# Layer 0's dense work in three passes, with unsplit weights, in place of two

## The chip, the cores and the metric

One core of one Trainium2 chip runs the whole program. The metric is the device time of one execution in microseconds (us). The kernel before took 3567.16 us (median of three runs, 3563.05 to 3572.27).

## The reference, cut to what matters

A decoder trunk of two layers over 512 tokens of 1024 features, in float32. Each layer has a token mixer and then a product-key retrieval of single experts:

```python
m  = x @ w_in                      # q, k, v | RG-LRU branch, its gate | 2 merge gates
ya = diff_attention(q, k, v, ...)  # 8 heads, two causal softmax maps each
yr = rg_lru(conv4(xr)) * gelu(gr)  # a recurrence along the tokens
y  = sigmoid(ga) * (ya @ w_br_attn) + sigmoid(gr) * (yr @ w_br_lru)
x  = layer_norm(alpha * x + y @ w_out)
# PEER: 8 heads x 16 of 16384 experts for each token
s1, i1 = top_k(q1 . keys1, 16); s2, i2 = top_k(q2 . keys2, 16)
e, g   = top 16 of the 256 sums s1 + s2, softmax over them
x  = layer_norm(alpha * x + sum_j g_j * gelu(x . u[e_j]) * v[e_j])
```

Every token needs 128 rows of `u` and of `v`, each of 1024 floats, in each layer. The tokens are causal: attention and the recurrence of a block of 128 tokens need the blocks before it, not those behind it. An expert phase needs only its own block's tokens and their choice.

## The kernel before, in words

The 512 tokens are four blocks of 128. Two streams of work are issued into one program (`run`, L752): `gathers()` and `dense()`.

**Gathers.** For each layer and block, `experts` (L682) issues 128 gathers (L730): one gather fetches, for each of 128 tokens, one row of `uv` (8 KB, `u` and `v` side by side), 1 MB in all, into one of 8 buffers (`self.gp`). There are 2 x 4 x 128 = 1024 gathers, numbered here from 0; gather 128 is the first of block 1. VectorE takes the dot product of the `u` half (L733), small operations on VectorE and ScalarE make a weight `w`, and the `v` half times `w` is added either by VectorE (`acc`, L703) or by TensorE (a diagonal of `w` on ScalarE at L707, then the product `pv` at L709). `self.share` sets which: a share of 0.7 means that seven of ten value rows go to VectorE.

**Dense work.** A pass over some blocks is `mixer` (L529 on: transposes, `attention` and `lru` woven together, two `merge`s, the output projection, a layer norm), then `route` (the scores and the choice of experts of the pass's first block), then `route_late` (the choice for its other blocks). A pass loads the layer's whole weights anew, chunk by chunk of 512 KB (`weight`, L195), whatever the number of its blocks: 80 chunks in the mixer (8 each for q, k, v, xr, gr, two gates, two branches, the output) and 16 in `route`. A chunk is 8 matmuls against activations of as many columns as the pass has tokens (`proj_T`, L220) or 8 for each block (`proj_N`, L242). Weights pass through 5 buffers.

**The first pass** (blocks 0 and 1 of layer 0) is special. Nothing can be gathered before its first experts are chosen. It is made with split operands: each weight chunk becomes two float32r parts (`split_weight`, L200: a copy on ScalarE, L204, a subtraction on VectorE, L205), activations likewise (`keep`), and a product is three passes of float32r matmuls, 24 to a chunk in place of 8.

**What sets the order.** `PLAN` (L53) gives for each pass the span of gathers over which it is spread: the gather at which the mixer starts, by which it ends and the scores begin, by which the first block's choice ends, by which the others' does. `run` steps whichever stream is behind. The framework then orders each engine's instructions, earlier-issued ones first among those that it takes to be ready; each engine runs its own list strictly in that order.

Of the kernel before, what the change touches and what calls it, by code (L numbers as in the profile page):

```python
# [17 lines left out]
AF = mybir.ActivationFunctionType  # L18
# [21 lines left out]
# chunk numbers in the packed weights  # L40
CH_Q, CH_K, CH_V, CH_XR, CH_GR, CH_GA, CH_GB = 0, 8, 16, 24, 32, 40, 48
CH_BA, CH_BL, CH_OUT, CH_WQ = 56, 64, 72, 80
# columns in the packed per-channel constants
# [3 lines left out]

# Issue order. The gathers of the experts' rows hold the time; the dense parts (some blocks of a
# layer's tokens, from the projections to the choice of experts) are issued between them, each over
# a span of gathers: (layer, blocks, first gather, gather by which the first block's scores begin,  # L50
# gather by which its experts are chosen, gather by which the others' are, shares of the value rows
# that the vector engine adds beside these three; the tensor engine adds the others).
PLAN = (  # L53
# [7 lines left out]
C_CHUNK = 1.75  # weight of 8 products of [128, 128] by [128, 128] in the issue order  # L61
HGS = {True: (1, 1, 2, 2, 2), False: (2, 2, 2, 2)}  # heads whose experts are chosen together


def weave(a, b, pace=1.0):
    """The steps of two generators by their costs, a's at so many times the pace of b's."""
    streams, clock = [iter(a), iter(b)], [0.0, 0.0]
    while streams[0] or streams[1]:
        i = 0 if not streams[1] or (streams[0] and clock[0] <= clock[1]) else 1
        c = next(streams[i], None)  # L70
        if c is None:
            streams[i] = None
        else:
            clock[i] += c / (1.0 if i else pace)
            yield c


class Acts:
    """Activations [features, tokens] that a product takes: as they are, or (hi, lo) in float32r
    parts whose sum they are."""  # L80
# [7 lines left out]
class Decoder:  # L88
# [18 lines left out]
    # ---------------------------------------------------------------- set-up  # L107
    def setup(self):
        nc, cp = self.nc, self.cp
        self.ident = cp.tile([P, P], F32, name="ident")  # L110
        make_identity(nc, self.ident)
        # base bias: B[p, m] = (m - 384) - p where that is <= 0, else a large negative
        W = S + P * (NB - 1)
        self.base = cp.tile([P, W], F32, name="base")
        nc.gpsimd.iota(self.base, pattern=[[1, W]], base=-P * (NB - 1), channel_multiplier=-1,
                       allow_small_or_imprecise_dtypes=True)
        nc.gpsimd.affine_select(out=self.base, in_=self.base, pattern=[[-1, W]],
                                compare_op=ALU.is_ge, fill=NEG, base=P * (NB - 1),
                                channel_multiplier=1)
        self.iota = cp.tile([P, NCAND], F32, name="iota")  # L120
        nc.gpsimd.iota(self.iota, pattern=[[1, NCAND]], base=0, channel_multiplier=0,
                       allow_small_or_imprecise_dtypes=True)
        self.lnrows = cp.tile([16, 512], F32, name="lnrows")
        self.junk_a = cp.tile([P, P], BF16, name="junk_a")
        self.junk_d = cp.tile([P, 4, HD], BF16, name="junk_d")

        ap = self.ap
        # tokens in two halves; the second's room serves the first dense part before
        self.xn, self.kT, self.vn = [None] * NB, [None] * 2, [None] * 2
        self.half_tiles(0)  # L130
        self.hist = ap.tile([P, KC, 3], F32, name="hist")
        self.hst = ap.tile([P, KC], F32, name="hst")
        self.e = [cp.tile([P, P], I32, name=f"e{b}") for b in range(NB)]
        self.g = [cp.tile([P, P], F32, name=f"g{b}") for b in range(NB)]
# [8 lines left out]
    def room(self, tag, dtype=F32, pool=None):  # L143
        """[128, 8, 256] for activations, in one of a few places."""
        t = (pool or self.ap).tile([P, 2 * D], dtype, name=f"room_{tag}", tag=tag)
        return t.rearrange("p (k n) -> p k n", k=KC)

    def layer_consts(self, l):
        nc, t1 = self.nc, self.t1
# [17 lines left out]
        # softplus(-lambda) = log1p(exp(-|lambda|)) + max(-lambda, 0)  # L167
# [26 lines left out]
    # ---------------------------------------------------------------- helpers  # L194
# [5 lines left out]
    def split_weight(self, hi, lo, l, ch):  # L200
        """A chunk's weights in float32r parts whose sum they are."""
        raw = self.wp.tile([P, D], F32, name="raw", tag="w")
        self.nc.sync.dma_start(raw, self.wpk[l, ch])
        self.nc.scalar.copy(hi, raw)  # L204
        self.nc.vector.tensor_tensor(lo, raw, hi.bitcast(F32), ALU.subtract)  # L205

    def proj_T(self, l, ch, act, n, ps=None):
        """[chunk columns, tokens] of (tokens) @ w."""
        if ps is None:
            ps = self.ps_mm.tile([P, 512], F32, name="ps_mm", tag="mm")  # L210
        if act.split:
            t = self.gp.tile([P, 2, D], F32R, name="wsp", tag="uv")
            self.split_weight(t[:, 0], t[:, 1], l, ch)
            hi, lo = (t[:, i].rearrange("p (k c) -> p k c", k=KC) for i in range(2))
            passes = ((hi, act.hi), (hi, act.lo), (lo, act.hi))
        else:
            passes = ((self.weight(l, ch), act.plain),)
        steps = [(w[:, kc, :], x[:, kc, :n]) for w, x in passes for kc in range(KC)]
        for i, (w, x) in enumerate(steps):
            self.nc.tensor.matmul(ps[:, :n], w, x, start=i == 0, stop=i == len(steps) - 1)  # L220
        return ps

    def proj_N(self, l, ch, act, blocks):
        """[tokens, block, chunk columns] of (tokens) @ w, for two chunks when act is split."""
# [22 lines left out]
    def keep(self, act, at, ps, scale=None):  # L247
        """act[at] <- ps (times scale, one per partition)."""
        nc = self.nc
# [25 lines left out]
    def layer_norm(self, l, which, rows, eps, junk):  # L275
        """in place on each xn[b] of rows (b, sums [128, k] that add up to its rows' sums); junk is
        written over."""
# [14 lines left out]
        # (x - mean) * gain, then * 1 / deviation + shift, gain and shift from PSUM  # L292
        for v, (col, op0, op1) in enumerate(((1, ALU.add, ALU.mult), (3, ALU.mult, ALU.add))):
# [5 lines left out]
            for (b, _), st in zip(rows, sts):  # L299
                # the result's halves leave one after the other  # L300
# [9 lines left out]
    # ---------------------------------------------------------------- mixer  # L310
    def attention(self, l, cst, blocks, x, ya, on):
        """The heads' projections run one head ahead of their softmax; on: room for the heads'
        outputs [tokens, head, (block, 128)] before their norms; it may be ya's."""
# [8 lines left out]
        def project(h):  # L322
            # the experts' accumulator lies idle in the first part
# [16 lines left out]
        def softmax(h, i, b, po, st):  # L340
# [24 lines left out]
            # c = -lam * sum1 / sum2  # L365
# [23 lines left out]
        def finish():  # L389
            """The heads' norms, all with one square root."""  # L390
# [30 lines left out]
    def lru(self, l, cst, blocks, x, yr):  # L421
# [6 lines left out]
        for g in range(KC):  # L428
# [30 lines left out]
            nc.scalar.activation(tha, tha, AF.Exp, scale=s4, bias=s4)          # a  # L459
            mu = t1.tile([P, W], F32, name="mu", tag="mu")[:, :n]  # L460
            nc.scalar.activation(mu, tha, AF.Square)
            # -expm1(2 log a) = -tanh(log a) (1 + a^2)
# [30 lines left out]
    def merge(self, l, blocks, x, ch_gate, ch_br, y, m, sofar, first):  # L493
        """The sum of (tanh(gate / 2) + 1) * (y @ w_br) over the two branches, twice the merged
        branches: the first's into sofar, both's into m."""
# [17 lines left out]
    def mixer(self, l, blocks, split):  # L513
# [31 lines left out]
        # xn <- 2 (alpha x + merged @ w_out); the layer norm takes the factor out through eps  # L545
# [18 lines left out]
    # ---------------------------------------------------------------- product keys  # L564
    def route(self, l, blocks):
        """The first block's experts are chosen as its scores come; the others' scores wait."""
# [52 lines left out]
    def top16(self, rows):  # L619
        """The 16 largest of each row of s, in order, with where they are, for each (s, values,  # L620
        places) of rows; s loses them."""
# [10 lines left out]
    def choose(self, l, h0, HG, sv, si, b):  # L632
        """Of the sums a + b only those with at most 16 pairs at or above them can be chosen."""
# [39 lines left out]
        # half the weight: the gelu of the experts leaves out its factor 1/2  # L673
# [7 lines left out]
    # ---------------------------------------------------------------- experts  # L681
    def experts(self, l, b, G=2):  # L682
# [4 lines left out]
        used = [0.0, False]  # the vector engine's share so far; whether the tensor engine began  # L687

        def finish(j0, dots, q, w, uvs):
            """from the dots to the weights, then the weighted sum of the value rows."""  # L690
# [61 lines left out]
    def run(self):  # L752
# [11 lines left out]
        def dense():  # L764
            """yields where in the gathers each step goes."""
            for l, blocks, j0, j1, j2, j3, shares in PLAN:
# [4 lines left out]
                for steps, total, a, b, share in (  # L771
                    (self.mixer(l, blocks, l == 0 and blocks[0] == 0),
# [32 lines left out]
def layout(inputs):  # L805
# [3 lines left out]
    def chunks(w):  # (L, 1024, n*128) -> (L, n, 128, 8*128)  # L809
        n = w.shape[2] // P  # L810
        return w.reshape(L, KC, P, n, P).transpose(0, 3, 2, 1, 4).reshape(L, n, P, KC * P)
# [25 lines left out]
```

## Time and profile before

| | |
|---|---|
| median of three runs | 3567.16 us (3563.05 to 3572.27) |
| span of the profiled execution | 3564.2 us |
| TensorE busy (PE) | 2963.9 us, 83% |
| VectorE busy (DVE) | 2883.3 us, 81% |
| ScalarE busy (ACT) | 1085.1 us, 30% |
| moved by the DMA engines | 1290.77 MB, mean 362 GB/s |
| of it by gathers (q0) | 1073.81 MB |
| of it weights, keys, tokens (q1) | 214.30 MB |

The profiled execution's own time is known by its span alone, 3564.2 us, 3.0 us under the median of the runs and within their spread. Busy time is by engine; PEld is TensorE's loading of stationary operands, which lies beside PE. PEclk is the granted clock of TensorE as a share of its full 2.4 GHz. A row of a table by stretch gives each engine's busy time and, in brackets, its number of instructions; on POOL these are gathers, so that the table counts them.

### The profile page before, as it was taken

The page shows a single profiled execution, that of the slowest core. Times are in us where ns is not written, and L with a number is a line of the kernel's source. Part 1 is how long each engine was busy: PE and PEld are TensorE (multiplying, and loading weights), DVE is VectorE, ACT ScalarE, POOL GpSimd, SP SyncE. Part 2 cuts the span into 40 slices and gives each one's busy share as a digit, 9 for nine tenths or more (in the row PEclk, how much of TensorE's full clock was granted, in tenths as well). Part 3 has the DMA queues.
Part 4 walks back from the last instruction along what each step waited for, and adds up shares of the span by engine and source line. Part 5 has one row for each costly group of instructions (what it writes and reads, how often), then busy time and mean ns, then how long its engine had stood idle before and what let it go on. Part 6 is the DMA issues. An engine that isn't in the chain of part 4 may idle for free.

```text
span 3564.2 us, 41600 instructions
## 1 busy us (share of the span) xinstructions
PE 2963.9 (83%) x11804; PEld 1907.9 (54%) x11804; DVE 2883.3 (81%) x9658; ACT 1085.1 (30%) x3174; POOL 1264.4 (35%) x1033
## 2 busy tenths in 40 slices
PE   8996878999999689999998689999898676655555
PEld 7995635677756346777654256677755222211111
DVE  7765799998768987777778977798778977788887
ACT  7842213442122234421222134432122121112111
POOL 0001234344332333333332443333333344456553
PEclk9997999999999889999999799999999889877777
DMA  6454889999999899999999899999999899999997
GB/s 200 159 167 178 299 326 384 390 411 416 418 385 366 341 362 403 390 375 387 395 396 365 296 409 395 371 409 418 418 382 349 298 394 421 421 421 407 422 421 318
DMA packets 219141, 1290.77 MB, mean 362 GB/s; under 512 B 24592, under 2 KB 37136, under 8 KB 87840
## 3 DMA queue, kind: packets, MB, share of 16 engines
q0 software_dynamic: 147456, 1073.81, 75.1%
q1 hardware_dynamic: 71456, 214.30, 16.1%
q8 instruction: 96, 1.57, 0.2%
q14 instruction: 133, 1.09, 0.1%
HBM read 1285.92 MB, written 2.10 MB: 361 GB/s over the span
## 4 chain that ended last, share of the span: by engine, by line
PE 35%; DVE 29%; DMA 20%; issue 8%; POOL 4%; ACT 4%; POOLq 0%; SPq 0%; DVEq 0%; ACTq 0%
DMA uvt<-uv_dram,e 20%; PE ps_mm L220 14%; PE pv L709 12%; DVE uvt L733 10%; DVE junk_d L660 5%; PE ps_mm L242 4%; POOL uvt L730 4%; DVE acc L703 3%; DVE si L627 1%; DVE sv L625 1%; PE ps_ln L297 1%; PE s L348 1%; PE pg L451 1%; PE ps_qk L220 1%; DVE ca L645 1%
## 5 line engine op out<-in xcount | busy, mean ns | idle before, releaser
L730 POOL DMA_INDIRECT uvt<-uv_dram,e x1024 | 1261.8, 1232 | 2268.7 <-DVE acc L703 598.8
L709 PE MATMUL pv<-uvt,dg 128*128 128x512 f32 x2588 | 1394.3, 680 | 483.3 <-ACT dg L707 481.9
L733 DVE SCALAR_TENSOR_TENSOR uvt<-uvt,xn 128x1024 f32<-128x1024 f32 x1024 | 1243.9, 1220 | 180.6 <-DMA uvt<-uv_dram,e 179.5
L709 PEld LDWEIGHTS pv<-uvt,dg 128*128 128x128 f32 x2588 | 521.0, 213 | 1206.7 <-ACT dg L707 703.2
L220 PE MATMUL ps_mm<-room_xT,w 128*128 128x256 f32 x3072 | 717.2, 382 | 3.4 <-ACT room_xT L252 2.9
L220 PEld LDWEIGHTS ps_mm<-room_xT,w 128*128 128x128 f32 x3072 | 576.5, 191 | 140.3 <-issue 58.6
L738 ACT ACTIVATE q<-dots 128x2 f32<-128x2 f32 x512 | 103.7, 203 | 1284.0 <-DVE uvt L733 1234.7
L703 DVE SCALAR_TENSOR_TENSOR acc<-uvt,w,acc 128x1024 f32<-128x1024 f32 x377 | 483.2, 1282 | 8.1
L707 ACT ACTIVATE dg<-ident,w 128x128 f32<-128x128 f32 x647 | 241.9, 397 | 184.7 <-DVE w L696 117.5
L660 DVE SCALAR_TENSOR_TENSOR junk_d<-iota,pf,ca 128x54 bf16<-128x54 f32 x1024 | 215.9, 268 | 0.4
L693 ACT ACTIVATE q<-q 128x2 f32<-128x2 f32 x512 | 103.7, 202 | 212.9 <-DVE q L691 204.3
L691 DVE SCALAR_TENSOR_TENSOR q<-q,dots 128x2 f32<-128x2 f32 x512 | 81.3, 159 | 103.2 <-ACT q L738 72.6
L696 DVE SCALAR_TENSOR_TENSOR w<-q,w 128x2 f32<-128x2 f32 x512 | 80.5, 157 | 88.0 <-ACT q L693 86.4
L205 DVE TENSOR_TENSOR wsp<-raw,wsp 128x1024 fp32r<-128x1024 f32 x96 | 116.2, 1221 | 18.3 <-ACT wsp L204 18.0
L220 PE MATMUL ps_mm<-room_xT,wsp 128*128 128x256 f32 x768 | 114.9, 292 | 0.5 <-ACT wsp L204 0.5
L204 ACT CAST wsp<-raw 128x1024 fp32r<-128x1024 f32 x96 | 98.7, 1047 | 20.1 <-issue 6.0
L220 PEld LDWEIGHTS ps_mm<-room_xT,wsp 128*128 128x128 f32 x768 | 102.0, 196 | 4.7 <-issue 2.4
L242 PE MATMUL ps_mm<-w,room_m 128*128 128x128 f32 x768 | 92.1, 282 | 6.9 <-DVE room_m L508 6.9
L242 PEld LDWEIGHTS ps_mm<-w,room_m 128*128 128x128 f32 x768 | 91.3, 198 | 12.0 <-DVE room_m L508 7.5
L242 PEld LDWEIGHTS ps_mm<-w,room_xT 128*128 128x128 f32 x768 | 92.6, 195 | 9.4 <-issue 7.7
L625 DVE MAX8 sv<-sc 128x8 f32<-128x128 f32 x128 | 36.5, 289 | 73.2 <-ACT sc L590 64.6
L242 PE MATMUL ps_mm<-w,room_xT 128*128 128x128 f32 x768 | 94.6, 278 | 0.0
(193 smaller groups left out, 3030.9 us busy)
## 6 DMA issues: line engine op xcount, KB each, us to landing
w<-wpk_dram SPq DMA_DIRECT2D x288, 512.0 KB
raw<-wpk_dram SPq DMA_DIRECT2D x96, 512.0 KB
uvt<-uv_dram,e POOLq DMA_INDIRECT x1024
gw<-gpk_dram SPq DMA_DIRECT2D x32, 128.0 KB
sk<-spk_dram SPq DMA_DIRECT2D x64, 64.0 KB
xn<-x_dram SPq DMA_DIRECT2D x4, 512.0 KB
out_dram<-xn SPq DMA_DIRECT2D x8, 256.0 KB
lq<-lqk_dram SPq DMA_DIRECT2D x2, 128.0 KB
```

The source lines that it names most:

```text
L204: self.nc.scalar.copy(hi, raw)
L205: self.nc.vector.tensor_tensor(lo, raw, hi.bitcast(F32), ALU.subtract)
L220: self.nc.tensor.matmul(ps[:, :n], w, x, start=i == 0, stop=i == len(steps) - 1)
L242: self.nc.tensor.matmul(out[:, i], x(slice(i * P, (i + 1) * P)), w, start=j == 0, stop=j == len(steps) - 1)
L660: nc.vector.scalar_tensor_tensor(out=self.junk_d[:, k % 4, :NCAND], in0=self.iota, scalar=pf[:, h, k : k + 1], in1=ca[:, 1, h], op0=ALU.is ...
L693: nc.scalar.activation(q, q, AF.Tanh, scale=C_GELU)
L703: nc.vector.scalar_tensor_tensor(out=acc, in0=t[:, D:], scalar=w[:, i : i + 1], in1=acc, op0=ALU.mult, op1=ALU.add)
L707: nc.scalar.activation(dg, self.ident, AF.Copy, scale=w[:, i : i + 1])
L709: nc.tensor.matmul(pv[:, half], dg, t[:, D + half * 512 : D + (half + 1) * 512], start=not used[1], stop=j == P - 2)
L730: nc.gpsimd.indirect_dma_start(out=t, out_offset=None, in_=self.uv, in_offset=bass.IndirectOffsetOnAxis(ap=e[:, j : j + 1], axis=0))
L733: nc.vector.scalar_tensor_tensor(out=t[:, :D], in0=t[:, :D], scalar=1.0, in1=x, op0=ALU.mult, op1=ALU.mult, accum_out=dots[:, i : i + 1])
L738: nc.scalar.activation(q, dots, AF.Square, scale=A_GELU)
```

## The change

`PLAN` gets three passes for layer 0: block 0 alone, block 1 alone, blocks 2 and 3. The mixer is told to work unsplit in all of them. The plan of layer 1 stays. Line numbers rise by one from L55 on. Comments went as well, which are left out here.

```diff
 PLAN = (
-    (0, [0, 1], 0, 0, 32, 64, (0.5, 0.0, 0.0)),
-    (0, [2, 3], 60, 205, 245, 360, (0.7, 0.0, 0.25)),
+    (0, [0], 0, 0, 30, 30, (0.5, 0.0, 0.0)),
+    (0, [1], 24, 96, 124, 124, (0.8, 0.2, 0.25)),
+    (0, [2, 3], 128, 215, 250, 365, (0.7, 0.0, 0.25)),
     (1, [0, 1], 258, 430, 485, 600, (0.7, 0.0, 0.25)),
     (1, [2, 3], 516, 690, 740, 860, (0.7, 0.0, 0.25)),
 )
...
                 for steps, total, a, b, share in (
-                    (self.mixer(l, blocks, l == 0 and blocks[0] == 0),
+                    (self.mixer(l, blocks, False),
                      80 * nb * C_CHUNK + 64 * nb + 12, j0, j1, shares[0]),
```

The first place in the order is TensorE at its start, behind the transposes of the tokens. Before, from the first key chunk (`ps_qk`) and the first recurrent chunk (`ps_mm`) on; `wsp` is a split weight, `room_xT` and `room_kT` the two parts of the tokens:

```order
L270 MATMUL ps_xt<-ident,xn_103 128x128 x16
L220 MATMUL ps_qk<-room_xT,wsp 128x256 x4
L220 MATMUL ps_mm<-room_xT,wsp 128x256 x4
L220 MATMUL ps_qk<-room_xT,wsp 128x256 x4
L220 MATMUL ps_qk<-room_kT_117,wsp 128x256 x4
L220 MATMUL ps_mm<-room_xT,wsp 128x256 x4
L220 MATMUL ps_mm<-room_kT_117,wsp 128x256 x3
L220 MATMUL ps_qk<-room_kT_117,wsp 128x256 x4
L220 MATMUL ps_qk<-room_xT,wsp 128x256 x8
```

Now, at the same place:

```order
L271 MATMUL ps_xt<-ident,xn_103 128x128 x8
L221 MATMUL ps_mm<-room_xT,w 128x128 x24
L452 MATMUL pg<-xc,gw 128x128 x2
L349 MATMUL s_270<-kT_104,qT_221 128x128
L243 MATMUL ps_mm<-w,room_xT 128x128 x8
L221 MATMUL ps_mm<-room_xT,w 128x128 x8
```

A chunk was 24 matmuls of 256 columns from split parts; it is 8 of 128 columns, and 24 of them are three whole chunks.

The second place is TensorE inside the attention of the pass over blocks 2 and 3, where `w` is a weight chunk, `uvt` a gathered row and `dg` its weight's diagonal. Before, up to the value product of gather 84 (`uvt_6100`) and on to that of gather 87 (`uvt_6182`):

```order
L379 MATMUL po_5958<-vn0_105,pr_6091 128x128 x2
L379 MATMUL po_5958<-vn1_5482,pr_6091 128x128 x2
L242 MATMUL ps_mm_6162<-w_6163,room_xT_5483 128x128 x16
L348 MATMUL s2_6204<-kT0_104,qT_6074 128x256
L709 MATMUL pv_3581<-uvt_6100,dg_6187 128x512 x2
L348 MATMUL s2_6204<-kT1_5481,qT_6074 128x128
L348 MATMUL s2_6204<-kT0_104,qT_6074 128x256
L348 MATMUL s2_6204<-kT1_5481,qT_6074 128x128
L451 MATMUL pg_6223<-xc_6216,gw_6131 128x256
L451 MATMUL pg_6226<-xc_6216,gw_6131 128x256
L220 MATMUL ps_mm_6239<-room_xT_5483,w_6240 128x256 x6
L709 MATMUL pv_3581<-uvt_6182,dg_6235 128x512 x2
```

Now, from behind the value product of gather 164 up to that of gather 167 (`uvt_7187`):

```order
L221 MATMUL ps_mm_7134<-room_xT_5700,w_7135 128x256 x8
L375 MATMUL pt_7164<-ident_88,pr_7095 128x128 x3
L221 MATMUL ps_mm_7174<-room_xT_5700,w_7175 128x256 x5
L380 MATMUL po_7088<-vn0_105,pr_7095 128x128 x2
L380 MATMUL po_7088<-vn1_5699,pr_7095 128x128
L221 MATMUL ps_mm_7174<-room_xT_5700,w_7175 128x256 x3
L349 MATMUL s2_7206<-kT0_104,qT_6961 128x256
L349 MATMUL s2_7206<-kT1_5698,qT_6961 128x256
L349 MATMUL s2_7206<-kT0_104,qT_6961 128x256
L349 MATMUL s2_7206<-kT1_5698,qT_6961 128x256
L221 MATMUL ps_mm_7226<-room_xT_5700,w_7227 128x256 x8
L710 MATMUL pv_5800<-uvt_7187,dg_7254 128x512 x2
```

The pass stands at later gathers, and more of its matmuls stand between two value products: in these rows 24 matmuls of weight chunks for three gathers, before 6 behind gather 84 and 16 of half the columns ahead of it.

## Rows read from the trace of the kernel before

**Rows 1.** The page: busy tenths, granted clock and transfers in 40 slices.

```profile
PE   8996878999999689999998689999898676655555
DVE  7765799998768987777778977798778977788887
PEclk9997999999999889999999799999999889877777
DMA  6454889999999899999999899999999899999997
GB/s 200 159 167 178 299 326 384 390 411 416 418 385 366 341 362 403 390 375 387 395 396 365 296 409 395 371 409 418 418 382 349 298 394 421 421 421 407 422 421 318
```

**Rows 2.** Busy time by stretch: start, layer norm and choice, gathers 0-127, 128-208, 209-368, rest.

```profile
core 0: us, PE busy (x) PEld busy (x) DVE busy (x) ACT busy (x) POOL busy (x), PEclk, DMA share, GB/s
0.00:287.00 287.00, 269.81 (x2124) 258.14 (x2124) 195.81 (x457) 186.58 (x367) 2.57 (x9) 1.00 0.53 172
287.00:320.00 33.00, 17.82 (x84) 13.79 (x84) 18.10 (x92) 10.58 (x20) 0.10 (x1) 0.67 0.02 5
320.00:763.00 443.00, 366.77 (x1580) 247.58 (x1581) 399.94 (x1657) 156.74 (x452) 159.04 (x128) 0.93 0.92 358
763.00:1032.00 269.00, 257.10 (x1200) 194.39 (x1199) 215.00 (x481) 71.30 (x212) 105.56 (x81) 0.97 0.99 405
1032.00:1579.00 547.00, 489.27 (x1831) 315.06 (x1830) 450.00 (x1887) 182.35 (x585) 193.13 (x160) 0.94 0.95 374
1579.00:3564.00 1985.00, 1563.10 (x4989) 878.91 (x4988) 1604.43 (x5088) 477.54 (x1539) 803.98 (x656) 0.89 0.97 387
```

**Rows 3.** The same table for two stretches with full transfers.

```profile
800.00:900.00 100.00, 99.94 (x469) 78.69 (x468) 87.76 (x187) 28.34 (x88) 45.67 (x32) 1.00 1.01 414
2400.00:2600.00 200.00, 186.50 (x870) 139.45 (x869) 160.85 (x355) 46.98 (x135) 70.75 (x59) 0.95 1.02 418
```

**Rows 4.** The order of time, TensorE: start us, us, engine, line, operation, tiles, shape, count.

```profile
216.24 1.12 PE L220 MATMUL ps_mm<-room_ya,wsp 128*128 128x256 f32 x8
978.52 10.89 PE L242 MATMUL ps_mm<-w,room_m 128*128 128x128 f32 x96
1515.70 3.72 PE L220 MATMUL ps_mm<-room_xT,w 128*128 128x256 f32 x16
```

**Rows 5.** TensorE's products at L220, then at L242, in the first 287 us.

```profile
0.00:287.00 287.00, 198.95 (x1536) 1.00 0.53 172
0.00:287.00 287.00, 47.79 (x384) 1.00 0.53 172
```

**Rows 6.** The order of time: the first split product, then up to the first gather.

```profile
14.89 1.23 PE L220 MATMUL ps_qk<-room_xT,wsp 128*128 128x256 f32 x4
...
288.74 1.15 ACT L285 ACTIVATE junk<-xn,ln_st 128x1024 f32<-128x1024 f32 x1
290.08 1.27 DVE L304 SCALAR_TENSOR_TENSOR xn<-xn,ln_st,ps_ln 128x1024 f32<-128x1024 f32 x1
319.90 1.09 POOL L730 DMA_INDIRECT uvt<-uv_dram,e  x1 [316.75 <-DVE sm_st L672]
```

**Rows 7.** Loads from SyncE (engine, operation, count, KB each) and the costliest groups.

```profile
w<-wpk_dram SPq DMA_DIRECT2D x288, 512.0 KB
L703 DVE SCALAR_TENSOR_TENSOR acc<-uvt,w,acc 128x1024 f32<-128x1024 f32 x377 | 483.2, 1282 | 8.1
L204 ACT CAST wsp<-raw 128x1024 fp32r<-128x1024 f32 x96 | 98.7, 1047 | 20.1 <-issue 6.0
L205 DVE TENSOR_TENSOR wsp<-raw,wsp 128x1024 fp32r<-128x1024 f32 x96 | 116.2, 1221 | 18.3 <-ACT wsp L204 18.0
```

**Rows 8.** Gathers 60 to 205: all engines, then TensorE's value products at L709 alone.

```profile
543.00:1025.00 482.00, 446.65 (x2087) 334.92 (x2086) 419.24 (x988) 169.81 (x478) 193.53 (x146) 0.96 0.99 400
543.00:1025.00 482.00, 106.07 (x213) 0.96 0.99 400
```

## The prediction

> **What bounds the kernel now.** I read the page's slices first, for where transfers run full and where not, then cut the span at the gathers (the table by stretch counts them on POOL), and priced single operations last. The slices [rows 1] show two regimes. For 320 us the DMA engines are about half busy: nothing can be gathered. Behind it they are mostly at 8 or 9 tenths, with dips where VectorE is at 9. The table [rows 2] gives the stages: gather 0 starts at 320, gather 128 at 763, gather 209 at 1032, gather 369 at 1579, and the rest takes 1985 us. Transfers reach 418 GB/s at their best with a pass running [rows 3]; the stages behind 320 run at 358, 405, 374 and 387. So the start is TensorE's (269.8 of 287 us busy, transfers at 172 GB/s), gathers 0 to 127 are held by VectorE (399.9 of 443) and TensorE (366.8) together, gathers 128 to 208 by transfers (405 of 418) with TensorE close behind (257 of 269). The plan of layer 1 is unchanged and the order of VectorE's and TensorE's work is equal for nearly all gathers behind 369. The forecast is therefore made of four stretches up to gather 369, against 1579 us.
>
> **1. The start, to gather 0.** Removed: 24 float32r matmuls to a chunk, 8 in 1.12 us, so 3.4 us [rows 4]; the split copies on ScalarE, 98.7 us in all [rows 7], nearly all here. Added: float32 chunks with 128 columns. A float32 matmul shows as two instructions, 96 of them in 10.89 us, 0.113 us each [rows 4]; a chunk has 16, 1.8 us; 80 chunks make 145 us. With 256 columns 16 take 3.72 us, so halving the columns halves the price. Everything else on TensorE in this stretch is 269.8 - 199.0 - 47.8 = 23 us for two blocks [rows 2, 5]; for one I take 17, as the transposes and gates have a floor per instruction. Sum 162 us, where it was 270. The first split product stood at 14.9 [rows 6]; without the split it waits for the load alone, and I take 10. What TensorE waited for on top was small (17 us idle in 287, most of it that start). Now each channel group's recurrence and each head's softmax has half the products to hide behind, and its chain on ScalarE and VectorE shrinks less than by half: I take 20 us of waits; the bounds are 7 (as now) and 55 (each of 16 chains uncovered by some 3.5 us). Layer norm to first gather takes 33 us now [rows 2]; one block less saves one square and one pass of 1.27 us in each step [rows 6] and some transposes: 28. Gather 0 at 10 + 162 + 20 + 28 = 220 us, bounds 205 and 255: **-100**.
>
> **2. Gathers 0 to 127.** Block 0's choice and the whole pass over block 1 are now here, with 107 weight chunks counted in the order of TensorE (39 before). 128 gathers of 1.049 MB and 107 loads of 0.524 MB, gates and keys with them, are 193 MB: 460 us at 418 GB/s. VectorE gains 14 value rows at 1.28 us [rows 7], since the shares are higher (66 on TensorE, counted in the order, 80 before), and loses about as much, as mixer work on 128 columns replaces a part on 256: still about 400. TensorE's sum falls a little (about 350). So transfers are the end that comes last here, where before it was VectorE; at the 405 of 418 GB/s that a transfer-bound stage reaches [rows 2] it is 475, and with the two choices, where VectorE is at 9 tenths, I take 480 (460 to 510). Before 443: **+37**.
>
> The added loads are where a rule of the Trainium skill speaks against the row. The stretch 2400 to 2600 moved 418 GB/s for 200 us [rows 3]. "DMA: Bandwidth & Descriptors", section Specifications, limits what one core draws from HBM to about 358 GB/s. By that these 193 MB would take 539 us and not 460, and the end would come some 60 us later than I forecast; by the row it doesn't hold on this core, so I keep 418.
>
> **3. Gathers 128 to 214.** The mixer of blocks 2 and 3 does not change, but it was spread over gathers 60 to 205 and is now over 128 to 215. In its stretch TensorE was busy 446.7 us of 482, of which 106.1 were value products [rows 8]: 340.6 us of dense work. Value products: 53 gathers in 213 instructions of four to a gather, 2.0 us a gather; 87 gathers with three of ten on TensorE add 52 us. So TensorE has 393 us of work here, while 87 gathers and 80 loads need 321 us of transfers at 418. TensorE becomes the bound. It was at most 96% busy over a long stretch (257 of 269, [rows 2]): 410 us; bounds 380 (no idle time, as in 800 to 900 [rows 3], and the full clock in place of 0.96) and 425 (at the 93% of [rows 8]). Before, gathers 128 to 208 took 269 us and six more at 547 / 160 = 3.42 us make 289.5: **+120**. This is the largest term, and the only one in which nothing is added; the work was hidden beside transfers and loses that cover.
>
> **4. Gathers 215 to 368.** Before 1579 - 1052.5 = 526.5 us. The choice for blocks 2 and 3 and the start of layer 1's first mixer follow, over ten gathers fewer than before (205 to 368 took 554 us). If those ten had been free it costs nothing, if they carried their share it costs 27: I take **+15**. Behind it: 0; cover there is unchanged, and I bound it by -10 and +10.
>
> Sum: -100 + 37 + 120 + 15 = +72. The profiled span is 3564.2, so 3636; the runs' median is 3.0 above the span, so about 3640. As a check by bytes: one more pass is 52 MB, 125 us at 418, against 100 us of transfers begun earlier: +25 even if every stretch were as well filled as now. The other 47 are the crowded mixer.
>
> **Rivals.** *The loads are free (faster).* Before, 443 us at 358 GB/s and 547 at 374 leave 64 + 58 us of transfer time unused. If the added pass fell into that, transfers alone would count: 1343 MB less 47 before gather 0 is 1296 MB. At the 383 GB/s that the kernel has now on average behind gather 0 (1241 MB in 3244 us) it ends at 205 + 3384 = 3590; with 395 at 205 + 3281 = 3486, about 3490. It decides from 388 GB/s on (gather 0 at 220). For it: the unused time is where the new loads go, and VectorE's load there is no greater. Against it: the crowded mixer, in which TensorE and not transfers is late, and which lowers the mean.
>
> *The start is bound by chains (slower still).* If the recurrences don't hide behind half the products, TensorE idles between chunks. In the 33 us behind the projections, where it was busy for 18, its granted clock was 0.67 [rows 2], so idle time makes the products behind it slower too. Half of the 162 us at 1.2 GHz is 81 us more: gather 0 at about 300, end at 3720. Against it: ScalarE loses 99 us of copies and VectorE most of 116 [rows 7], so that both are busy for little over half of the stretch. The Trainium skill ("TensorE: Matmul & The Clock Gate", Part 1) says that the throttled clock is the default and that activity releases it; with it the whole 162 us could double, the trace's busy start had 1.00.
>
> *The change cancels out.* Start at 205, stretch 2 at 460, stretch 3 at 380, stretch 4 unchanged: 1572, so 3560: every term at its favourable end at once.
>
> That the change doesn't do what it says is excluded by the order: no split weight is left, and block 1's pass stands among gathers.
>
> **How the numbers follow.** The forecast has 0.79, the chains 0.10, free loads 0.05, cancelling out 0.05, the page's limit 0.01, as the row speaks against it. About 0.3% (11 us) is what a measurement of this kernel can tell from no change. Slower by more: 0.79 + 0.10 + 0.01 = 0.90; within: 0.04; faster: 0.06 (the free loads, and a little of cancelling out). The forecast's own spread: start -15 to +35, stretch 2 -20 to +30, stretch 3 -30 to +15, stretch 4 -15 to +12, the rest 10 either way; they don't go together, so I take -50 to +55: 3590 to 3695, which leaves out most of the rivals and some of the forecast's tails.
>
> **What would show it.** In the new profile: gather 0 at 205 to 255 with TensorE at 8 or 9 tenths before it; gather 128 at about 700, transfers near 400 GB/s in between where they were 358; from 128 to 215 over 4.5 us for a gather, TensorE above 95% and transfers at some 330 GB/s; gather 369 at about 1650; from there on 1985 us within 10. It is wrong if gather 215 comes before 1050, which would mean that products of blocks 2 and 3 ran beside block 1's gathers, or if gather 0 comes after 280.

## The result

The changed kernel takes 3678.42 us (median of four runs, 3671.45 to 3687.7) against 3569.05 us before (3563.05 to 3572.27): a ratio of 1.0315 (95% interval 1.0295 to 1.0336), 109 us slower. Forecast was slower by 72.

The page of the profiled execution (span 3676.8 us, 113 above that of before) in slices of 92 us, to be laid beside [rows 1]:

```profile
PE   8978777799999968999899669999989666656555
DVE  4278857898645897787678987798777987788887
PEclk9989998899999989999999889999999879877777
DMA  7789998898787989999899899999999899999997
GB/s 255 270 320 401 415 416 343 343 379 322 273 298 291 350 353 368 397 379 385 346 397 365 326 352 399 384 389 418 418 392 366 304 361 418 422 421 410 421 422 324
```

The half-busy start is gone and transfers reach 415 GB/s in slices 4 and 5 (counted from 0); but slices 10 to 12 have 273 to 298 GB/s with TensorE at 9, where before there were 366 to 418. The table by stretch, cut at the same gathers as [rows 2] (start, layer norm and choice, gathers 0-127, 128-214, 215-368, rest; the columns are PE, PEld, DVE, ACT, POOL, then clock, DMA share, GB/s):

```profile
0.00:175.00 175.00, 163.00 (x1350) 155.35 (x1351) 60.24 (x282) 76.00 (x213) 2.56 (x9) 1.00 0.80 263
175.00:205.00 30.00, 25.11 (x158) 20.44 (x157) 13.91 (x94) 7.97 (x18) 0.14 (x1) 0.83 0.51 159
205.00:712.00 507.00, 388.82 (x2219) 290.39 (x2219) 394.93 (x1694) 142.44 (x473) 153.48 (x128) 0.95 0.96 382
712.00:1141.00 429.00, 394.94 (x1961) 311.21 (x1960) 298.37 (x689) 143.26 (x389) 109.02 (x87) 0.96 0.83 312
1141.00:1673.00 532.00, 477.00 (x1827) 310.07 (x1826) 436.06 (x1853) 179.76 (x570) 182.49 (x154) 0.96 0.94 366
1673.00:3676.00 2003.00, 1571.65 (x5029) 882.87 (x5028) 1603.63 (x5092) 478.86 (x1549) 790.87 (x656) 0.89 0.96 384
```

| stretch | before | forecast | measured | term forecast | term measured |
|---|---|---|---|---|---|
| to gather 0 | 320 | 220 | 205 | -100 | -115 |
| gathers 0-127 | 443 | 480 | 507 | +37 | +64 |
| gathers 128-214 | 289.5 | 410 | 429 | +120 | +139 |
| gathers 215-368 | 526.5 | 541.5 | 532 | +15 | +6 |
| the rest | 1985 | 1985 | 2003 | 0 | +19 |

The second stretch, cut once more at gathers 32 and 96, shows where it lost its transfers:

```profile
205.00:316.00 111.00, 90.35 (x416) 59.71 (x416) 92.25 (x579) 29.73 (x105) 32.79 (x33) 0.94 0.98 381
316.00:576.00 260.00, 193.29 (x1341) 160.24 (x1340) 190.47 (x467) 85.59 (x264) 85.25 (x65) 0.98 1.02 415
576.00:712.00 136.00, 105.18 (x463) 70.45 (x464) 112.21 (x649) 27.12 (x104) 35.44 (x32) 0.89 0.85 321
```

From 316 to 576, in block 1's mixer, transfers are full. TensorE waits there for weight chunks above all (engine, tile, line; releaser; total us, times, longest us):

```profile
PE ps_mm L221 <- DMA w<-wpk_dram: 42.0, 29, 1.8
PE ps_mm L243 <- DMA w<-wpk_dram: 5.0, 4, 1.8
```

Between 430 and 560 weight chunks make up 80% of the chain of work that ended last; they land 13 to 18 us after the step that let them start. Some of its longest pieces (start, duration, what):

```profile
423.02 18.24 DMA w<-wpk_dram
443.39 13.95 DMA w<-wpk_dram
459.54 16.64 DMA w<-wpk_dram
480.08 14.26 DMA w<-wpk_dram
498.23 7.16 PE ps_mm L221 x64
505.40 13.48 DMA w<-wpk_dram
521.07 13.21 DMA w<-wpk_dram
```

From 576 on, in block 1's choice, nothing is full: 321 GB/s, TensorE 105 and VectorE 112 of 136 us. Among TensorE's waits there is one that the kernel before has nowhere in its trace, for the small loads of sub-keys:

```profile
PE ps_sc L585 <- DMA sk<-spk_dram: 13.1, 3, 7.0
PE pv L710 <- ACT dg L708: 11.9, 7, 6.9
```

In gathers 128 to 214 the next gather waits on POOL above all for a buffer whose value product stands in TensorE's list behind dense matmuls:

```profile
POOL uvt L731 <- PE pv L710: 161.5, 22, 19.1
POOL uvt L731 <- DVE acc L704: 91.2, 27, 10.1
```

Before, beside the same mixer (543 to 1025, gathers 60 to 205), it was the other way round:

```profile
POOL uvt L730 <- DVE acc L703: 175.2, 62, 6.7
POOL uvt L730 <- PE pv L709: 58.7, 25, 16.8
```

The last six gathers of the stretch, 209 to 214, took 69 us, where before they took 20. TensorE worked off the rest of the mixer there (the stretch in a row, then the longest piece of its chain):

```profile
1073.00:1141.00 68.00, 64.70 (x377) 52.67 (x376) 21.04 (x73) 8.16 (x22) 5.42 (x6) 0.95 0.62 221
1104.76 17.86 PE ps_mm L243 x160
```

### The profile page after: what moved, and what is told of

The parts are those of the page before. It is cut to its first block, busy times and chain, and to the rows that moved or that the text cites. A ratio compares the mean times of both kernels' runs of the same rounds, so it can differ in the third digit from the quotient of the medians.

```text
span 3676.8 us, 43366 instructions
## 1 busy us (share of the span) xinstructions
PE 3020.5 (82%) x12536; PEld 1970.3 (54%) x12536; DVE 2807.2 (76%) x9700; ACT 1028.3 (28%) x3210; POOL 1238.6 (34%) x1033
## 4 chain that ended last, share of the span: by engine, by line
PE 33%; DMA 25%; DVE 24%; issue 10%; POOL 4%; ACT 3%; POOLq 0%; SPq 0%; DVEq 0%; ACTq 0%
DMA uvt<-uv_dram,e 19%; PE ps_mm L221 14%; PE pv L710 12%; DVE uvt L734 8%; DMA w<-wpk_dram 5%; DVE junk_d L661 4%; PE ps_mm L243 4%; POOL uvt L731 4%; DVE acc L704 3%; DMA sk<-spk_dram 1%; DVE si L628 1%; PE ps_ln L298 1%; DVE sv L626 1%; PE s L349 1%; PE ps_sc L585 1%
## 5 line engine op out<-in xcount | busy, mean ns | idle before, releaser
L710 PE MATMUL pv<-uvt,dg 128*128 128x512 f32 x2512 | 1348.3, 678 | 424.0 <-ACT dg L708 423.0
L221 PE MATMUL ps_mm<-room_xT,w 128*128 128x256 f32 (+1 forms) x5120 | 982.6, 343 | 45.3 <-DMA w<-wpk_dram 34.4
L221 PEld LDWEIGHTS ps_mm<-room_xT,w 128*128 128x128 f32 x5120 | 828.0, 194 | 201.3 <-issue 86.9
L221 PE MATMUL ps_mm<-room_ya,w 128*128 128x256 f32 (+1 forms) x640 | 121.9, 344 | 10.7 <-DVE mth L505 5.7
L243 PE MATMUL ps_mm<-w,room_xT 128*128 128x128 f32 x1024 | 127.3, 280 | 3.0 <-DMA w<-wpk_dram 2.1
L221 PE MATMUL ps_mm<-room_yr,w 128*128 128x256 f32 (+1 forms) x640 | 122.0, 339 | 8.3 <-DMA w<-wpk_dram 7.9
L243 PEld LDWEIGHTS ps_mm<-w,room_xT 128*128 128x128 f32 x1024 | 122.6, 195 | 11.1 <-issue 6.9
L221 PEld LDWEIGHTS ps_mm<-room_ya,w 128*128 128x128 f32 x640 | 104.3, 194 | 28.1 <-DVE mth L505 7.4
L221 PEld LDWEIGHTS ps_mm<-room_yr,w 128*128 128x128 f32 x640 | 102.3, 191 | 24.1 <-issue 8.2
L695 DVE TENSOR_TENSOR w<-dots,g 128x2 f32<-128x2 f32 x512 | 80.0, 156 | 22.7 <-ACT dg L708 11.8
```

The costliest lines, as they stand in the source:

```text
L243: self.nc.tensor.matmul(out[:, i], x(slice(i * P, (i + 1) * P)), w, start=j == 0, stop=j == len(steps) - 1)
L710: nc.tensor.matmul(pv[:, half], dg, t[:, D + half * 512 : D + (half + 1) * 512], start=not used[1], stop=j == P - 2)
```

## Experiments

The theory: the time is lost in gathers 0 to 223, about half by the loads of an additional pass, where transfers are the bound, and half by the crowding of the mixer of blocks 2 and 3, where TensorE is; the earlier start pays part of it. The rivals: the loads are hidden; the crowding is, or is only moved by another plan; the missing split is what costs. Ratios are to the kernel before, run beside on the same chip (3562 to 3566 us). Times are medians; stretches and gathers are read from the one profiled execution, which lies up to 10 us above the median.

**Two passes, no split** (before, with that part alone changed).

```diff
-                    (self.mixer(l, blocks, l == 0 and blocks[0] == 0),
+                    (self.mixer(l, blocks, False),
```

> The kernel before with the split of its first pass alone undone (two passes, blocks 0 and 1 together, float32 chunks of 256 columns). Theory: the start is TensorE's. A chunk of 16 instructions of 256 columns takes 3.7 us where the split one took 3.0 to 3.4, so 80 chunks make 296 us against 247; gather 0 moves from 320 to 360-375 us and the end with it, about 3567 + 50 = 3617 us. Rival: the split's copies on ScalarE and VectorE held the start; then gather 0 stays at or before 320 us and the time is 3567 us or less.

3583.33 us, 1.0064 (1.0047 to 1.0081). Gather 0 came at 366, as the theory said, but the end is only 21 us late:

```profile
0.00:366.00 366.00, 349.87 (x1844) 298.92 (x1844) 112.97 (x453) 120.66 (x295) 2.57 (x9) 0.97 0.42 137
366.00:781.00 415.00, 373.11 (x1486) 249.92 (x1486) 389.51 (x1655) 152.70 (x450) 157.32 (x128) 0.95 0.96 385
```

Gathers 0 to 127 took 415 us and not 443. So the split gains 46 us before the first gather and costs 28 behind it: 14 of the 16 chunks of the first choice, split too, stand among gathers there. Expected were 50 us at the end, 21 came. In two passes, then, the missing split doesn't explain 109 us; three passes with a split were not run.

**One load for block 1's pass.** The result is another one; 95 loads are left out.

```diff
     def weight(self, l, ch):
+        if self.reuse and self.kept is not None:
+            return self.kept
...
+        self.kept = w
...
+                self.reuse, self.kept = blocks == [1], None
```

> The changed kernel, with one weight chunk loaded for the pass over block 1 and used for all of its 96 chunks (its result is another one; 95 loads of 0.5 MB are left out). Theory: gathers 0 to 127 are bound by transfers, the added loads among them. 95 loads are 50 MB, 119 us at 418 GB/s; VectorE, with 395 us of work, is the next bound at about 440 us for the stretch in place of 508, so gather 128 comes at about 645 us in place of 712 and the end at about 3613 us (3595 to 3630). Rival: the stretch is held by the two choices of experts and by TensorE's waits, and the loads are hidden; then the end stays within 15 us of 3678 us.

3612.05 us, 1.0141 (1.0124 to 1.0158): 66 us earlier than the changed kernel. The first 128 gathers took 453 us (129 on POOL with the next one), transfers no longer full, VectorE at 87%:

```profile
202.00:655.00 453.00, 384.49 (x2220) 288.15 (x2218) 394.24 (x1697) 143.36 (x474) 156.40 (x129) 0.95 0.86 319
```

The loads are paid, at 54 us in this stretch. Gather 128 came at 655 and not at 645, and some 8 us more were gained behind it, so that the end meets the expected 3613 us partly by luck. VectorE (87%) and TensorE (85%) are next, and not VectorE alone: in the mixer's part, 420 to 527, TensorE is at 94%. With another result block 1 also gathers other rows; that this changed the speed of gathers is not excluded, but late in the span both kernels move 421 GB/s.

**Fewer, and more, value rows on TensorE beside the last mixer of layer 0.**

```diff
-    (0, [2, 3], 128, 215, 250, 365, (0.7, 0.0, 0.25)),
+    (0, [2, 3], 128, 215, 250, 365, (0.9, 0.0, 0.25)),   # the first; the second: 0.4
```

> The changed kernel with nine of ten value rows (0.9 in place of 0.7) on VectorE beside the mixer of blocks 2 and 3. Theory: TensorE is the bound of gathers 128 to 214. In gathers 128 to 223, 16 value products fewer (26 in place of 42, counted in the order) at 2.0 us take 32 us off TensorE, and VectorE (298 of 429 us) has room for 16 x 1.28 us: the end comes 20 to 35 us earlier, about 3648 us. Rival: the stretch is bound by transfers or by the buffers of the gathers; then the end stays within 10 us of 3678 us.

> The changed kernel with four of ten value rows (0.4 in place of 0.7) on VectorE beside the mixer of blocks 2 and 3. Theory: TensorE is the bound there; 23 value products more in gathers 128 to 223 (65 in place of 42) at 2.0 us add 46 us, the end comes 35 to 50 us later, about 3720 us. Rival: VectorE or transfers are the bound; VectorE loses 23 x 1.28 us of work and the end comes 0 to 15 us earlier.

Fewer: 3629.26 us, 1.0187 (1.0170 to 1.0204), 49 us earlier. More: 3685.41 us, 1.0345 (1.0328 to 1.0362), 7 us later. The stretch of 87 gathers, fewer and then more:

```profile
714.00:1110.00 396.00, 365.79 (x1889) 298.49 (x1890) 309.83 (x707) 140.60 (x377) 108.36 (x88) 0.95 0.87 338
716.00:1162.00 446.00, 428.85 (x2077) 328.84 (x2076) 277.22 (x665) 155.50 (x418) 95.71 (x87) 0.98 0.82 301
```

With fewer, TensorE has 29 us less work and the stretch is 33 us shorter, and the stretches behind it gain too: 13 us in the profiled execution. With more it has 34 us more work and the stretch is only 17 us longer: TensorE's busy share rises from 92 to 96%. So it is the bound, but not all of the 429 us were its work; some 17 us were idle time that more work fills (the longest single waits there are for VectorE's softmax and for a value row's diagonal). That "more" would cost 35 to 50 us was wrong. Up to gather 209 it did: gathers 128 to 208 took 306, 360 and 412 us with fewer, as changed and with more. The last six gathers took 89, 69 and 34 us. So it looks as if gathers that run ahead of the mixer wait for what is left of it at the end; this was not tested by itself.

**Another plan for the same three passes**, alone and with the share of 0.9.

```diff
-    (0, [0], 0, 0, 30, 30, (0.5, 0.0, 0.0)),
-    (0, [1], 24, 96, 124, 124, (0.8, 0.2, 0.25)),
-    (0, [2, 3], 128, 215, 250, 365, (0.7, 0.0, 0.25)),
+    (0, [0], 0, 0, 16, 16, (0.5, 0.0, 0.0)),
+    (0, [1], 14, 70, 100, 100, (0.8, 0.2, 0.25)),
+    (0, [2, 3], 98, 215, 250, 365, (0.7, 0.0, 0.25)),    # with the share: 0.9
```

> The changed kernel with an earlier plan for the same three passes: block 0's choice over gathers 0 to 16, block 1 over 14 to 100, blocks 2 and 3's mixer over 98 to 215. Theory: most of the loss is the crowding of the last mixer, not the third pass. Gathers 0 to 127 need 483 us of transfers (500 to 520 us), in gathers 128 to 223 TensorE's work falls from 426 to 340 us (sums from the order), about 362 us; gather 224 comes 85 to 100 us earlier than in the changed kernel and the end at 3575 to 3605 us. Rival: the third pass itself costs the time, by its loads and its second choice; then spreading only moves it, and the end stays within 25 us of 3678 us.

> The same with nine of ten value rows on VectorE beside the mixer of blocks 2 and 3. Theory: TensorE's work in gathers 128 to 223 falls to 314 us and that of VectorE stays below it, so that the stretch takes about 340 us: 3545 to 3590 us, about the time of the kernel before, as the sum by bytes (one more pass of loads, 125 us, against 115 us of transfers begun earlier) would have it. Rival: VectorE, at 9 tenths in the first 128 gathers, becomes the bound and it is no better than the plan alone (3575 to 3605 us or later).

Alone: 3645.26 us, 1.0229 (1.0212 to 1.0247), 33 us earlier; neither the 73 to 103 of the theory nor at most the rival's 25. Gathers 0 to 127 took 530 us and not 500 to 520, and gather 224 came 21 us earlier and not 85 to 100. With the share: 3604.13 us, 1.0108 (1.0091 to 1.0125), 74 us earlier, still slower than before and outside the 3545 to 3590 us expected; the rival, no better than the plan alone, failed by 41 us. Gathers 0 to 223 in the changed kernel, and in this last one:

```profile
205.00:1171.00 966.00, 813.22 (x4286) 620.06 (x4286) 708.12 (x2424) 295.11 (x890) 272.73 (x225) 0.96 0.90 350
205.00:1108.00 903.00, 756.31 (x4167) 599.24 (x4166) 731.80 (x2458) 285.71 (x861) 269.24 (x225) 0.94 0.95 375
```

Crowding is real, and the sum was too hopeful in taking one engine's work for the time: 756 us of TensorE's and about 810 of transfers (903 us at 375 GB/s, were they at 418) need 903. That each is the late one in turn fits this, and was not tested by itself.

**Buffers for the sub-keys.**

```diff
-                sk = t2.tile([P, 2, P], F32, name="sk", tag="gs")[:, 0]
+                sk = t2.tile([P, P], F32, name="sk", tag="sk", bufs=3)
```

> The changed kernel with three buffers of their own for the sub-keys in place of two shared with the gates. Theory: in the choice of block 1 (gathers 104 to 127) TensorE waits 13 us for loads of sub-keys that stand behind gathers in the transfer queues, 10 more in block 0's; a third buffer hides most of it, gather 128 comes 8 to 20 us earlier and the end at 3658 to 3670 us. Rival: the stretch is held by VectorE's choice; the wait is only turned into another one and the end stays within 6 us of 3678 us.

3658.33 us, 1.0260 (1.0242 to 1.0277): 20 us earlier, but not by the way of the theory. TensorE waits for sub-keys nearly as long as without the buffers, here in the choices of blocks 0 and 1 (204 to 316 and 570 to 710; it was 9.8 and 13.1 us in the changed kernel):

```profile
PE ps_sc L585 <- DMA sk<-spk_dram: 10.1, 4, 5.2
PE ps_sc L585 <- DMA sk<-spk_dram: 10.8, 4, 3.4
```

In the profiled execution gather 128 comes 8 us earlier, gather 215 only 2.5, gather 369 only 3, and the end 11. So the gain at gather 128 was mostly lost again, and what makes the kernel faster is not explained; the edit also leaves the gates' buffers to the gates alone.

**The plan, the share and one load together.** Another result again.

> The three passes with the earlier plan and nine of ten value rows on VectorE in the last mixer (3604 us), and one weight chunk loaded for the whole pass over block 1 (95 loads of 0.5 MB left out, another result). Theory: crowding and loads are two separate costs; with the first eased, the loads are what is left. 119 us of transfers fewer in gathers 0 to 127, where they are the bound from gather 32 on: the end 45 to 75 us earlier, 3530 to 3560 us, at or below the kernel before (3564). Rival: crowding and loads were paid in the same wait; then with the crowding eased the loads are hidden and the end stays within 15 us of 3604 us.

3545.32 us, 0.9944 (0.9926 to 0.9963): 59 us earlier than with the loads. Eased crowding doesn't hide them; they cost 66 and 59 us in the two settings, and the crowding that plan and share ease costs 74 us with the loads and 67 without them. The two add up: 133 us together. Even so the kernel is only 21 us faster than the one before, though its gathers start some 115 us earlier: gathers 0 to 223 take 844 us, before 766, and what stands behind them 17 us more. What holds these last 78 us was not separated.

**The first choice unsplit**, in the kernel before; its mixer stays split. The first experiment pointed to it.

```diff
         yield 6.0 * nb
+        if split:
+            x = self.acts_x = Acts(self.room("xT"))
         for i, b in enumerate(blocks):
             self.transpose_x(x, i, b)
```

> The kernel before with its first mixer split as it is, and the tokens for its choice of experts unsplit, so that the 16 chunks there are loaded and used as float32. Theory: in the two-pass kernel without any split, gathers 0 to 127 took 415 us in place of 443, because the 14 split chunks among them no longer take buffers of the gathers, 17 us of VectorE and 14 us of ScalarE; this gain is kept here, the start stays at 320 us, and the end comes 10 to 28 us earlier, about 3542 us, which beats both kernels. Rival: the 28 us came from elsewhere (TensorE's full clock there, or rooms that come free earlier); then the end stays within 6 us of 3562 us.

3534.00 us, 0.9920 (0.9906 to 0.9935): faster than both kernels, and 31 us faster than the kernel before beside it, a little more than the 10 to 28 expected. The start is kept at 319 us, gathers 0 to 127 take 421 us in place of 443:

```profile
0.00:319.00 319.00, 294.92 (x2228) 277.11 (x2228) 209.00 (x544) 195.94 (x388) 2.57 (x9) 0.98 0.48 157
319.00:740.00 421.00, 375.38 (x1486) 250.57 (x1487) 389.84 (x1653) 152.15 (x450) 153.47 (x128) 0.95 0.96 380
```

With the sub-keys' buffers on top:

> The two-pass kernel with unsplit tokens in its first choice of experts (3534 us), and three buffers of their own for the sub-keys. Theory: waits for sub-keys belong to passes over one block, where a chunk's product takes 1.8 us and not 3.7; in the two-pass kernel's trace TensorE never waits for them, so nothing changes: within 6 us of 3534 us. Rival: the third buffer frees the queue of loads in every pass (it gained 20 us in the three-pass kernel, half of it behind gather 128); then the end comes 8 us or more earlier.

3532.08 us, 0.9910 (0.9889 to 0.9931): no change against 3534, as expected. In the traces read, TensorE waits for sub-keys only in the choice of a pass over one block.

## Why the prediction was right, and where its terms were off

The direction, the mechanism of the three large terms and their order held; 72 us were forecast and 109 measured. That the sum came this near is in part luck: gathers 0 to 127, 128 to 214 and the rest together cost 65 us more than forecast, and the start and gathers 215 to 368 cost 25 us less.

- **The start** gained 15 us more than forecast: TensorE's 163 us of work in 175 agree with 10 + 162, but the 20 us of waits between chunks did not come; the chains of recurrence and softmax stayed hidden behind half the products (TensorE waited under 4 us for ScalarE and VectorE there). The rival of chains and a low clock fell with it (granted clock 1.00).
- **Gathers 0 to 127**: the bytes were right (193 MB forecast, 382 GB/s over 507 us are 194), and so was the bound (415 GB/s for 260 us), but the allowance for the choices was not. 475 us were forecast without them, 5 more for both; block 1's choice alone ran at 321 GB/s, 136 us for what would be 105 at 415, and block 0's at 381, 111 us for 102. That step is mis-sized by 27 us. The waits for sub-keys lie there; that a chunk of 1.8 us is too short to cover them fits, but was not tested. TensorE's work was 389 us and not about 350, and the kernel before made the products of 48 chunks among these gathers, not 39; no term rests on either.
- **Gathers 128 to 214**: TensorE's work was forecast at 393 us and measured 395. The step from work to time took a busy share of 96%; it was 92%, below the 93% of the stated bound, and 429 us lie 4 above it. A sign named for this stretch, TensorE above 95%, did not show. The experiments with the share show both sides of it: work sets the stretch, and there was idle time in it. The expectation that products of 2 us simply add up failed in one direction.
- **Behind gather 215** 15 us were forecast and 25 measured, 6 of them in gathers 215 to 368 and 19 behind, where the forecast had 0 and allowed 10. Of these 16 lie in gathers 369 to 415 (176 us, before 160); the three-pass kernels all show 169 to 176 there, the two-pass ones 160 to 162. That TensorE enters layer 1's first mixer with a backlog fits, but wasn't tested.
- **Free loads** fell: loads cost 59 to 66 us. So did, with one core of the chip at work, the limit of 358 GB/s from the Trainium skill ("DMA: Bandwidth & Descriptors", Specifications): this trace holds 415 GB/s for 260 us.

## What to carry to other kernels

A transfer-bound kernel that starts its transfers earlier by reading its weights once more gains the idle start and pays the bytes; count both, then count what the later passes lose of the span that hid them, which was the largest term here. An engine's work divided by its best busy share is a lower bound where two engines and the transfers are all near full; in the stretches here the time lay 4 to 15% above the largest sum. And a trick that serves a stretch where an engine is idle (the split) should end where that stretch ends: carried on beside the gathers it cost 22 to 28 us in gathers 0 to 127.

## What had not been expected of the hardware

In block 1's mixer, with transfers at 415 GB/s, a weight load of 512 KB took 13 to 18 us to land, for a chunk that TensorE works off in 1.8 us. The first such load of the program, before any gather, took 7.4 us (2.59 to 9.94). In block 1's choice, at 321 GB/s, loads of sub-keys of 64 KB stood in the chain for 9 to 11 us each, and TensorE waited up to 7 us for one. That the small loads wait behind gathers in the queues fits these times; no run took the gathers away to show it.
